# One of four layers: RWKV-7's pairs of heads in a fixed table of ticks, TensorE in program order, and the triangular inverse kept on chip

## The chip, the cores and the metric

The kernel runs on one core of one Trainium2 chip. The metric is the time of one execution in device microseconds, as the median of several executions. A profiled execution gives a trace of every instruction on the engines: TensorE (PE, with its weight loads as PEld), VectorE (DVE), ScalarE (ACT), GpSimd (POOL) and the DMA queues that SyncE (SP) feeds.

## The reference, cut to what matters

A trunk of four layers works on 512 prompt tokens and 32 sample tokens (8 sequences of 4), 544 columns in all. Its mixers are HGRN2, RWKV-7, Mamba-2 and HGRN2, and each is followed by a SwiGLU network. The change is in the second layer, RWKV-7, which has 16 heads of 64 rows:

```python
rkv = jnp.einsum('nbtd,nde->nbte', xs[:3], w_rkv)
...
def step(s, inp):
    r_t, w_t, k_t, v_t, kk_t, a_t = inp
    sa = jnp.einsum('bhvk,bhk->bhv', s, -kk_t)
    s = (s * w_t[:, :, None, :] + sa[..., None] * (kk_t * a_t)[:, :, None, :]
         + v_t[..., None] * k_t[:, :, None, :])
    return s, jnp.einsum('bhvk,bhk->bhv', s, r_t)
...
o = ((o - mean) * lax.rsqrt(var + RW_GN_EPS)).reshape(b, t, d) * lnx_w + lnx_b
bonus = jnp.sum(r * k * r_k, axis=-1, keepdims=True) * v
o = (o + bonus.reshape(b, t, d)) * gate
y = o.astype(h.dtype) @ w_out
...
x = x + out
x = x + _swiglu(_rmsnorm(x, p['norm_ffn'][i]), p['ffn_w_gate'][i], p['ffn_w_up'][i], p['ffn_w_down'][i])
```

The recurrence is computed in chunks of 64 tokens. Within a chunk the steps depend on one another through a strictly triangular 64x64 matrix for each head, and the kernel inverts one minus that matrix.

## The kernel before, in words

All activations lie with 128 of the 1024 features on partitions and tokens in columns. A product of float32 accuracy is made of three matmuls in a reduced format: a weight and an activation are each split into a high part (`whi`, `nh`) and a remainder (`wlo`, `nl`), and the products high by high, remainder by high and high by remainder are added up in PSUM. A weight tile of 128x1024 is loaded into `wraw` (three buffers), copied to `whi` by ACT (two buffers) and subtracted to `wlo` by DVE (two buffers); it then serves 24 matmuls.

The RWKV layer runs in this order. First come the projections that the keys need. Then `_rwkv_main` goes over eight objects `_Pair`: a pair is two tiles of 128 rows, hence four heads, on one half of the prompt (256 tokens, four chunks). The first four pairs are the four feature quarters of the first half, the other four those of the second half. Each pair has a `front` and a `back`:

- `front` computes `keys` for both tiles (decay scans, normalised keys, the tiles `AR` and `BKF`), the scores of keys against keys and receptances, several transposes by TensorE (`turn`), and then `inverse`. The 64x64 triangles are cut into 32x32 blocks, and these into 16x16 blocks. The 16x16 diagonal blocks go through DRAM (`nd`, then `nb`) into a layout of 64 blocks on 64 partitions, DVE solves them by 14 steps of a multiply (`pr`) and a reduction (`tb`), the result goes through DRAM again (`img`, then `TI`), and TensorE joins 16 to 32 and 32 to 64.
- `back` goes over the four chunks in a chain: products with the state carried from the chunk before, then the new state `zz` and the output `pso`. Its matmuls for output and state contract over 128 rows, in which the two kinds of rows of a head are put side by side (`SO`, `UV`, `TK`). A norm over each head (`head_norm`) and `finish` close it, tile by tile.

Beside these pairs there is work of large matmuls which does not depend on them at that time. `_rv` is the projection of receptance and value: 768 matmuls of 272 columns, needed pair by pair (line 931 of the profile). `_rwkv_end` on the first half of the prompt is the output projection and the SwiGLU network: 1776 matmuls of 256 columns (line 264), which need the first four pairs' outputs. In the text both are called products. They are emitted between the pairs in portions (`FILL`) and at a low priority, and a scheduler at build time decides by its own estimate where in each engine's queue every instruction stands. After the pairs come `_Samples` (the 32 sample tokens, with small and DVE-heavy work), the rest of the first half's products, and the tail: `_rwkv_end` on the second half with the samples, 288 columns.

Of the kernel before, what the change touches and what calls it, by code (L numbers as in the profile page):

```python
# [26 lines left out]
class Core:  # L27
# [217 lines left out]
class Part:  # L245
# [11 lines left out]
    def mm(self, w, xs):  # L257
# [19 lines left out]
    def out_proj(self, src, acts):  # L277
        for m in range(KD):
            ps = self.mm(self.k.weights(src[m], KD, P), acts)
# [16 lines left out]
    def ffn(self, layer):  # L296
# [3 lines left out]
        yield  # L300
        for g0, gn in FGRP:
            hid = []
            for m in range(g0, g0 + gn):
                ps = self.mm(k.weights(io["ffn_gate"][layer, m], KD, P), xs)
# [5 lines left out]
                yield  # L310
                ps = self.mm(k.weights(io["ffn_up"][layer, m], KD, P), xs)
                V.tensor_tensor(out=g, in0=g, in1=ps, op=ALU.mult)
                hid.append(self.halves(g, "a", m - g0))
                yield
            for m in range(KD):
                ps = self.mm(k.weights(io["ffn_down"][layer, m, :, g0:g0 + gn], gn, P), hid)
# [4 lines left out]
                yield  # L321
# [300 lines left out]
LEAD = 1  # L622
SETS = 3
FILL = (3, 2, 2, 2, 5, 3, 10, 18, 18, 18)
PRIO = 800
LOW = 4000
ENDS = 78
# [5 lines left out]
class Rwkv:  # L633
# [11 lines left out]
    def _rwkv_ffn(self, layer, rp, dp, p1, early):  # L645
        tc, nc = self.tc, self.nc
        with self.scope("rw", dict(s="01", m="2", u="e")) as pool:
# [9 lines left out]
            with tc.tile_pool(name="rw3p", bufs=1) as p3:  # L657
# [17 lines left out]
    def _rwkv_end(self, layer, part, st):  # L675
# [4 lines left out]
        yield  # L680
# [3 lines left out]
    def _rwkv_proj(self, layer, rp, p1, px, dp):  # L684
# [75 lines left out]

        z = p1.tile([P, T], F32, tag="st", name="z", bufs=3)
        G.memset(z, 0.0)
        st["img"] = []
        for j in range(8):
            t = dp.tile([8, 4, 1056], F32, name=f"img{j}")
            nc.sync.dma_start(out=t.rearrange("c b x -> (c b x)").rearrange("(p a) -> p a", p=P), in_=z[:, 0:264])
            st["img"].append(t)
# [94 lines left out]
    def _rwkv_consts(self, rp, dp):  # L862
# [7 lines left out]
        c = dict(msk=load("rmask", [P, P]), m16=load("mask16", [P, 32]), blk=load("blk", [P, P]))  # L870
# [4 lines left out]
        c["tb"] = [rp.tile([64, 16, 16], F32, name=f"tb{i}") for i in range(2)]  # L875
        for t in c["tb"]:
            nc.gpsimd.affine_select(out=t, in_=self.ones[0:64, 0:1].rearrange("p (a b) -> p a b", a=1).to_broadcast([64, 16, 16]),
                                    compare_op=ALU.is_equal, fill=0.0, base=0, pattern=[[1, 16], [-1, 16]], channel_multiplier=0)
        c["nd"] = [dp.tile([8, 4, 1056], F32, name=f"nd{i}") for i in range(3)]
        return c  # L880

    def _rwkv_main(self, layer, st, c, p2):
        carry = p2.tile([P, KD, 64], F32, name="carry")
        out = [self.xp.tile([P, T], F32, tag=f"x{m}", name="o") for m in range(KD)]
# [4 lines left out]
        proj = self._rv(st)  # L889
        end = self._rwkv_end(layer, part, st)  # L890

        def fill(gen, n):
            with self.tc.high_priority(offset=-LOW):
                for _ in range(n):
                    next(gen, None)

        for _ in range(FILL[0]):
            next(proj)
        ahead = []
        for j in range(8 + LEAD):  # L900
            if j < 8:
                ahead.append(_Pair(self, j, st, c, p2, carry))
                ahead[-1].front()
# [986 lines left out]
```

## Time and profile before

| | |
|---|---|
| Median of three executions | 3569.36 us (3558.92 to 3569.93) |
| The profiled execution | 3567.21 us, its span 3565.4 us |
| Mean granted TensorE clock, share of full speed | 0.955 |
| TensorE busy | 3357.3 us, 94% of the span |
| DVE, ACT, POOL busy | 2220.4, 1417.2 and 850.7 us |
| Pairs of the RWKV layer | 929.70 to 1413.30 us |
| Samples' chain | 1430.70 to 1527.60 us |
| Tail (second half's output projection and network) | 1593.50 to 1867.60 us |

The rows are from one profiled execution. A row with a colon between two times is a stretch of the span; the numbers behind it are its length, and for each engine busy time and (x) instructions, then the granted clock of TensorE as a share of full speed (0.5 is 1.2 GHz, 1.0 is 2.4 GHz) and the DMA's share. A row that begins with one time is an instruction or a run of alike instructions in order of time: its start, its duration, its line, what it writes and reads. Matmuls overlap, so the step from one start to the next says what one costs in a stream.

### The profile page before, as it was taken

How to read it: one execution, taken by the hardware profiler on the slowest of the kernel's cores; microseconds unless marked ns; L12 is line 12 of the kernel's file. 1: busy time of each engine (PE TensorE's matmuls, PEld its weight loads, DVE VectorE, ACT ScalarE, POOL GpSimd, SP SyncE). 2: the span in 40 equal slices, each digit the busy share in tenths (PEclk: the TensorE clock that was granted, in tenths of full speed). 3: DMA queues.
4: the chain of work that ended last, by engine and by line, in shares of the span. 5: the costliest groups of instructions: out<-in, count | busy, mean ns of one | idle time of the engine just before them, and what ended most of it. 6: DMA issues, size and time to landing. Idle time of an engine off the chain costs nothing. (4 is left out here: it accounts for less than half of the span.)

```text
span 3565.4 us, 75773 instructions
## 1 busy us (share of the span) xinstructions
PE 3357.3 (94%) x31593; PEld 3164.1 (89%) x31593; DVE 2220.4 (62%) x3714; ACT 1417.2 (40%) x2404; POOL 850.7 (24%) x930
## 2 busy tenths in 40 slices
PE   8998999999989889999998889999999999899998
PEld 7887999998877778799998778999999988799998
DVE  7787543467466665776667988763444778754345
ACT  4444422235546555245343333342223544442223
POOL 5564100022123331211003543210000466410001
PEclk9998999999968889999999989999999999899999
DMA  3222322244644323554444444332222322232223
GB/s 122 81 80 86 128 89 87 87 136 151 198 122 119 108 77 122 174 187 145 160 152 115 136 130 146 117 101 89 89 86 92 116 90 83 91 119 89 89 89 108
DMA packets 226246, 409.29 MB, mean 115 GB/s; under 512 B 66273, under 2 KB 130145, under 8 KB 225905
## 3 DMA queue, kind: packets, MB, share of 16 engines
q1 hardware_dynamic: 225904, 404.45, 35.1%
q8 instruction: 249, 4.08, 0.5%
q14 instruction: 93, 0.75, 0.1%
HBM read 357.25 MB, written 46.51 MB: 113 GB/s over the span
## 5 line engine op out<-in xcount | busy, mean ns | idle before, releaser
L62 ACT ACTIVATE whi<-wraw 128x1024 fp32r<-128x1024 f32 (+2 forms) x585 | 596.9, 1022 | 1371.3 <-issue 745.1
L64 DVE TENSOR_TENSOR wlo<-wraw,whi 128x1024 fp32r<-128x1024 f32 (+2 forms) x585 | 708.3, 1212 | 199.3 <-ACT whi L62 194.0
L93 PE MATMUL big<-nl,whi 128*128 128x256 f32 (+1 forms) x3600 | 764.5, 292 | 0.0
L93 PE MATMUL big<-nh,wlo 128*128 128x256 f32 (+1 forms) x3600 | 758.4, 291 | 2.9 <-DVE wlo L64 2.9
L93 PE MATMUL big<-nh,whi 128*128 128x256 f32 (+1 forms) x3600 | 753.7, 289 | 3.0 <-DVE raw L1482 1.8
L93 PEld LDWEIGHTS big<-nh,whi 128*128 128x128 f32 x3600 | 584.0, 190 | 11.8 <-issue 7.4
L93 PEld LDWEIGHTS big<-nl,whi 128*128 128x128 f32 x3600 | 583.4, 190 | 8.6 <-issue 7.0
L93 PEld LDWEIGHTS big<-nh,wlo 128*128 128x128 f32 x3600 | 579.7, 190 | 11.9 <-issue 6.3
L130 POOL TENSOR_TENSOR acc<-acc,sq 128x256 f32<-128x256 f32 (+1 forms) x126 | 122.0, 968 | 1663.6 <-ACT sq L129 1662.4
L212 DVE TENSOR_TENSOR fg<-fg,big 128x544 f32<-128x544 f32 x66 | 47.6, 721 | 235.4 <-PE big L93 232.9
L264 PE MATMUL psp<-nh,whi 128*128 128x256 f32 x592 | 177.0, 299 | 5.4 <-ACT whi L62 4.4
L264 PE MATMUL psp<-nh,wlo 128*128 128x256 f32 x592 | 175.9, 297 | 5.4 <-DVE wlo L64 5.2
L264 PE MATMUL psp<-nl,whi 128*128 128x256 f32 x592 | 175.3, 297 | 0.0
L208 DVE TENSOR_TENSOR fg<-big,rs 128x544 f32<-128x544 f32 x66 | 47.8, 724 | 199.4 <-PE big L93 188.7
L221 DVE TENSOR_TENSOR fd<-big,rs 128x544 f32<-128x544 f32 (+2 forms) x96 | 55.5, 580 | 176.4 <-PE big L93 159.5
L93 PE MATMUL big<-hh,wlo 128*128 128x256 f32 (+1 forms) x768 | 158.8, 288 | 0.0
L93 PE MATMUL big<-hl,whi 128*128 128x256 f32 (+1 forms) x768 | 158.1, 287 | 0.0
L93 PE MATMUL big<-hh,whi 128*128 128x256 f32 (+1 forms) x768 | 157.9, 287 | 0.0
L264 PE MATMUL psp<-x,whi 128*128 128x288 f32 x704 | 143.2, 298 | 0.0
L264 PEld LDWEIGHTS psp<-nh,whi 128*128 128x128 f32 x592 | 118.1, 199 | 11.8 <-ACT whi L62 7.0
L264 PEld LDWEIGHTS psp<-nh,wlo 128*128 128x128 f32 x592 | 118.0, 199 | 11.8 <-DVE wlo L64 7.2
L264 PEld LDWEIGHTS psp<-nl,whi 128*128 128x128 f32 x592 | 118.0, 199 | 6.2 <-issue 4.9
(620 smaller groups left out, 7390.9 us busy)
## 6 DMA issues: line engine op xcount, KB each, us to landing
wraw<-in_ffn_gate SPq DMA_DIRECT2D x110, 512.0 KB, 3.2
wraw<-in_ffn_up SPq DMA_DIRECT2D x110, 512.0 KB, 3.2
wraw<-in_ffn_down SPq DMA_DIRECT2D x80, 512.0 KB, 3.5
wraw<-in_hg_in SPq DMA_DIRECT2D x64, 512.0 KB, 3.3
wraw<-in_ffn_down SPq DMA_DIRECT2D x64, 384.0 KB, 3.1
wraw<-in_rw_in SPq DMA_DIRECT2D x40, 512.0 KB, 3.8
wraw<-in_mb_in SPq DMA_DIRECT2D x40, 512.0 KB, 3.4
wraw<-in_hg_out SPq DMA_DIRECT2D x32, 512.0 KB, 3.2
```

The source lines that it names most:

```text
L62: nc.scalar.activation(out=hi, in_=raw, func=AF.Copy)
L64: nc.vector.tensor_tensor(out=lo, in0=raw, in1=hi.bitcast(F32), op=ALU.subtract)
L93: self.nc.tensor.matmul(out=ps[0:cols, HALF[h]], lhsT=a[:, k, c0:c0 + cols], rhs=b[:, HALF[h]], start=first, stop=last)
L130: (eng or nc.gpsimd).tensor_tensor(out=acc, in0=acc, in1=sq, op=ALU.add)
L208: V.tensor_tensor(out=g, in0=pg, in1=rs, op=ALU.mult)
L212: V.tensor_tensor(out=g, in0=g, in1=pu, op=ALU.mult)
L221: V.tensor_tensor(out=d[:, c], in0=ps[:, c], in1=rs[:, c], op=ALU.mult)
L264: self.k.nc.tensor.matmul(out=ps, lhsT=a[:, i], rhs=b, start=first, stop=last)
```

## The change

Every TensorE instruction of the layer's helpers now goes through `mm`, and while `ordered` is set it is pinned in the order in which the program emits it. `_rwkv_main` emits in ten slots of 12 ticks. In slot s the `back` of pair s-2, the inverse (`inv`) of pair s-1 and the `front` of pair s each advance by one step in each tick, and behind them a tick gets its share of the products. A quantum is six matmuls. 24 quanta of the projections stand ahead of the first slot, 104 are spread over slots 0 to 5, and slots 6 to 9 get five quanta of the first half's output work in each tick. The inverse starts from the identity plus the matrix's entries inside 2x2 blocks and joins blocks of 2, 4, 8 and 16 in four rounds on chip, each of 2 times 32 matmuls of 32x32, an addition and a transpose on DVE; the two trips through DRAM and the 14 steps on 64 partitions are gone. The heads' matmuls use the 64 rows of their own head only: one K=128 product becomes two of K=64 (`SK` with `VT`, `SB` with `U`). The head norm works on both tiles at once.

```diff
+    ordered = False
+
+    def mm(self, **kw):
+
+        i = self.nc.tensor.matmul(**kw)
+        if self.ordered:
+            self.tc.keep_in_program_order(i)
...
-                self.k.nc.tensor.matmul(out=ps, lhsT=a[:, i], rhs=b, start=first, stop=last)
+                self.k.mm(out=ps, lhsT=a[:, i], rhs=b, start=first, stop=last)
+            if i % 2 and i < n - 1:
+                yield 0
...
-LEAD = 1
-SETS = 3
-FILL = (3, 2, 2, 2, 5, 3, 10, 18, 18, 18)
-PRIO = 800
 LOW = 4000
+TICKS = 12
+PROJ = (24, 6)
+PART = 5
 ENDS = 78
...
-                    for _ in range(ENDS - KD - sum(FILL[4 + LEAD:])):
-                        next(end)
-                    tail = self._rwkv_end(layer, part, st)
-                    for _ in range(KD + 2):
-                        next(tail)
-                    for _ in end:
-                        pass
-                for _ in tail:
-                    pass
+                    end.steps(ENDS - KD)
+                    tail = _Steps(self._rwkv_end(layer, part, st))
+                    tail.steps(KD + 2)
+                    end.steps(ENDS)
+                tail.steps(ENDS)
...
+        c["XI"] = [p2.tile([P, 8, 64], F32, name=f"XI{i}") for i in range(2)]
+        for t in c["XI"]:
+            self.nc.gpsimd.memset(t, 0.0)
...
-        proj = self._rv(st)
-        end = self._rwkv_end(layer, part, st)
-
-        def fill(gen, n):
-            with self.tc.high_priority(offset=-LOW):
-                for _ in range(n):
-                    next(gen, None)
-
-        for _ in range(FILL[0]):
-            next(proj)
-        ahead = []
-        for j in range(8 + LEAD):
-            if j < 8:
-                ahead.append(_Pair(self, j, st, c, p2, carry))
-                ahead[-1].front()
-            if j < 5:
-                fill(proj, FILL[1 + j])
-            if j >= LEAD:
-                ahead.pop(0).back()
-            if j >= 3 + LEAD:
-                fill(end, FILL[1 + j])
+        proj = _Steps(self._rv(st))
+        end = _Steps(self._rwkv_end(layer, part, st))
+        pairs = [_Pair(self, j, st, c, p2, carry) for j in range(8)]
+        self.ordered = True
+        proj.quanta(PROJ[0])
+        front, inv = pairs[0].front(), None
+        next(front)
+        quota = 128 - PROJ[0]
+        for s in range(10):
+            work = [g for g in (pairs[s - 2].back() if s >= 2 else None, inv, front) if g is not None]
+            front = inv = None
+            for t in range(TICKS):
+                for g in work:
+                    next(g, None)
+                if t == 7 and s < 7:
+                    front = pairs[s + 1].front()
+                    next(front)
+                n = s * TICKS + t
+                if s < PROJ[1]:
+                    proj.quanta(quota * (n + 1) // (PROJ[1] * TICKS) - quota * n // (PROJ[1] * TICKS))
+                else:
+                    end.quanta(PART)
+            for g in work:
+                for _ in g:
+                    pass
+            if s < PROJ[1] <= s + 1:
+                proj.quanta(128)
+            if s < 8:
+                inv = pairs[s].inv()
+                next(inv)
+        self.ordered = False
...
+                        if k in (1, 3, 5):
+                            yield 0
                     t = self.tmps("sq", 3)[:, 0:RV]
                     nc.scalar.copy(out=t, in_=ps)
                     nc.sync.dma_start(out=st[name][m][:, cols], in_=t)
-                yield
+                    yield 1
...
+            ps = [psb("s", [P, 4, 2, 64]) for _ in range(2)]
+            for a in (1, 0):
+                for q, e in each:
+                    mm(out=flat(ps[a][rows[e], q]), lhsT=BK[rows[e], q, a], rhs=flat(AR[rows[e], q]), start=True, stop=True)
+            SW = [til(f"SW{a}", [P, 4, 64]) for a in range(2)]
+            for a in (1, 0):
+                V.tensor_tensor(out=SW[a], in0=ps[a][:, :, 0], in1=mask(0), op=ALU.mult)
+            for a, t in ((1, self.SK), (0, self.SB)):
+                V.tensor_tensor(out=t[:, i], in0=ps[a][:, :, 1], in1=mask(64), op=ALU.mult)
...
-        for b in range(4):
-            nc.sync.dma_start(out=rowsof(nd, b), in_=NNf[quarter[b]])
-        nb = til("nb", [nb_, 16, 16], 2)
-        nc.sync.dma_start(out=nb, in_=blocks(nd))
-        tb = c["tb"][self.j % 2]
-        V.tensor_copy(out=tb[:, 1, 0:1], in_=nb[:, 0:1, 1])
-        for t in range(2, 16):
-            pr = til("pr", [nb_, 15, 15], 2)
-            V.tensor_tensor(out=pr[:, 0:t, 0:t], in0=nb[:, 0:t, t].rearrange("p (o j) -> p o j", o=1).to_broadcast([nb_, t, t]),
-                            in1=tb[:, 0:t, 0:t].rearrange("p j s -> p s j"), op=ALU.mult)
-            V.tensor_reduce(out=tb[:, t, 0:t], in_=pr[:, 0:t, 0:t], axis=mybir.AxisListType.X, op=ALU.add)
-        nc.sync.dma_start(out=blocks(img), in_=tb)
-        TI = til("TI", [P, n2, 32], 2)
-        for b in range(4):
-            nc.sync.dma_start(out=TI[quarter[b]], in_=rowsof(img, b))
...
+        M = til("ML", [P, 4, n2, 32])
+        X, TI = til("X", [P, n2, 32], 2), til("TI", [P, n2, 32], 2)
+        G.tensor_tensor(out=X, in0=flat(self.NN), in1=c["lmask"][:, 1:2].to_broadcast([P, n2, 32]), op=ALU.mult)
+        G.tensor_tensor(out=X, in0=X, in1=c["lmask"][:, 0:1].to_broadcast([P, n2, 32]), op=ALU.add)
+        G.tensor_tensor(out=M, in0=flat(self.NN).rearrange("p (o c) t -> p o c t", o=1).to_broadcast([P, 4, n2, 32]),
+                        in1=c["lmask"][:, 2:6].rearrange("p l (o t) -> p l o t", o=1).to_broadcast([P, 4, n2, 32]), op=ALU.mult)
+        V.transpose(out=lines(TI), in_=lines(X))
...
-        Y = til("Y", [P, n2, 32], 2)
-        ACT.copy(out=Y, in_=quads(M, TI, own))
-        V.tensor_tensor(out=X, in0=X, in1=quads(Y, X, own), op=ALU.add)
-        T32 = TI
-        V.transpose(out=T32.rearrange("p c t -> p (c t)"), in_=X.rearrange("p c t -> p (c t)"))
+        for l in range(4):
+            Y = til("Y", [P, n2, 32], 2)
+            ACT.copy(out=Y, in_=quads(M[:, l], TI, own))
+            yield
+            V.tensor_tensor(out=X, in0=X, in1=quads(Y, X, own), op=ALU.add)
+            V.transpose(out=lines(TI), in_=lines(X))
+            if l < 3:
+                yield
...
+            for i in range(2):
+                for x, a, first in ((VT, 1, True), (U, 0, False)):
+                    for e in range(2):
+                        mm(out=pp[rows[e], i], lhsT=TK[rows[e], i, q, a], rhs=x[rows[e], i, q], start=first, stop=not first)
...
+                terms = [(VT[:, i, q], self.SK[:, i, q]), (U[:, i, q], self.SB[:, i, q])]
                 if z is not None:
...
-                for i, e in both:
-                    PE.matmul(out=pp[rows[e], i], lhsT=TK[e][:, i, q], rhs=UV[e][:, i, q], start=True, stop=True)
...
-                        PE.matmul(out=po[rows[e], i, q], lhsT=UV[e][:, i, q], rhs=SO[e][:, i, q], start=True, stop=z is None)
```

On TensorE, this is a place in the fourth of the pair slots after the change (`L75` is the helper `mm`; `psp` takes a product, `zz,XA` is the chain of `back`, `TI,ML` a round of the inverse, `bn,blk` the bonus sum of `front`):

```order
L75 MATMUL psp<-nh_9646,wlo 128x272
L75 MATMUL psp<-nl_9647,whi 128x272
L75 MATMUL psc<-zz,XA 64x64 x4
L75 MATMUL psm<-TI,ML 32x32 x32
L75 MATMUL pss<-bn,blk 128x256
L75 MATMUL psp<-nh_9648,whi 128x272
L75 MATMUL psp<-nh_9648,wlo 128x272
L75 MATMUL psp<-nl_9649,whi 128x272
```

The same kinds of work in the kernel before, where a pair's chain and another pair's inverse meet (`L1183`, `L1188`, `L1196` and `L1199` are the chain, `L1141` the inverse, `L1057` scores, `L264` a product):

```order
L1183 MATMUL psc<-zz,XA 64x64 x4
L1141 MATMUL psm<-TI,NN 32x32 x3
L952 MATMUL pss<-bn,blk 128x256
L1141 MATMUL psm<-TI,NN 32x32 x22
L1196 MATMUL pso<-SO_12939,UV_12943 64x64
L1141 MATMUL psm<-TI,NN 32x32 x4
L1188 MATMUL psc<-UV_12943,TK_12941 64x64
L1188 MATMUL psc<-UV_12944,TK_12942 64x64
```

A stage of the inverse that was cut up by the chain's matmuls stands in one piece after the change, behind the chain's step and ahead of the tick's products, and nothing can pass a matmul whose input is late.

On DVE, this is the start of one pair's 14 steps in the kernel before (`pr` and `tb`), with other pairs' work between:

```order
L1120 COPY tb_10730<-nb 64x1
L1014 SCALAR_TENSOR_TENSOR kn<-lk,rvec,rk 128x256
L1123 TENSOR_TENSOR pr<-nb,tb_10730 64x2x2
L1125 TENSOR_REDUCE tb_10730<-pr 64x2
L1123 TENSOR_TENSOR pr<-nb,tb_10730 64x3x3
L1125 TENSOR_REDUCE tb_10730<-pr 64x3
L1123 TENSOR_TENSOR pr<-nb,tb_10730 64x4x4
L968 TENSOR_TENSOR fd<-fd,fs 128x256
```

After the change, at the place where the projections turn from the first 272 columns to the next (`nl` is the remainder of a new input, `X` and `TI` are the inverse, `zz` the chain, `wlo` a weight's remainder):

```order
L1217 TENSOR_TENSOR zz<-zd,psc 128x128
L1054 SCALAR_TENSOR_TENSOR bn<-lr,rvec,la 128x256
L69 TENSOR_TENSOR nl_9649<-sq,nh_9648 128x272
L1157 TENSOR_TENSOR X<-X,psm 128x256
L69 TENSOR_TENSOR nl_9651<-sq,nh_9650 128x272
L1158 STREAM_TRANSPOSE TI<-X 128x256
```

The short steps are replaced by one addition and one transpose for each round; at the turn of the projections the sixteen remainders stand among the steps of the inverse and the chain.

## Rows read from the trace of the kernel before

**Rows 1.** Four stretches: the pairs, the last pair's finish, the samples, the remaining products.

```profile
929.70:1413.30 483.60, 433.95 (x5534) 372.12 (x5535) 301.10 (x749) 268.83 (x559) 138.33 (x243) 0.82 0.42 120
1413.30:1430.70 17.40, 13.20 (x97) 11.68 (x96) 9.22 (x18) 10.02 (x14) 6.57 (x8) 1.00 0.41 130
1430.70:1527.60 96.90, 90.18 (x814) 73.26 (x815) 76.04 (x115) 31.14 (x45) 31.37 (x37) 0.95 0.56 180
1527.60:1593.50 65.90, 62.95 (x508) 61.78 (x507) 45.22 (x72) 29.05 (x42) 2.61 (x7) 0.97 0.55 187
```

**Rows 2.** The pairs' stretch from 991.60, cut where the granted clock changes.

```profile
991.60:1104.30 112.70, 100.86 (x1327) 83.36 (x1326) 67.12 (x185) 56.94 (x135) 26.26 (x53) 0.62 0.40 107
1104.30:1189.60 85.30, 76.46 (x1046) 64.19 (x1044) 59.14 (x148) 54.73 (x115) 32.71 (x52) 0.98 0.44 125
1189.60:1346.60 157.00, 136.94 (x1896) 114.33 (x1895) 97.33 (x270) 85.59 (x182) 55.51 (x89) 0.75 0.33 89
1346.60:1413.30 66.70, 63.87 (x796) 58.92 (x796) 40.43 (x75) 39.08 (x62) 8.51 (x12) 1.00 0.38 123
```

**Rows 3.** Two of these stretches, TensorE's instructions of line 931 (projections) alone.

```profile
991.60:1104.30 112.70, 32.05 (x129) 25.40 (x129) 0.62 0.40 107
1104.30:1189.60 85.30, 36.46 (x228) 30.90 (x228) 0.98 0.44 125
```

**Rows 4.** TensorE in order of time, clock full, small work and then products.

```profile
1348.51 0.75 PE L1141 MATMUL psm<-TI,NN 32*32 32x32 f32 x64
1349.19 0.70 PE L952 MATMUL psu<-o,blk 128*128 128x256 f32 x2
1349.54 0.47 PE L264 MATMUL psp<-nh,whi 128*128 128x256 f32 x1
1349.85 0.28 PE L264 MATMUL psp<-nh,wlo 128*128 128x256 f32 x1
1349.96 0.28 PE L264 MATMUL psp<-nl,whi 128*128 128x256 f32 x1
1350.08 0.28 PE L264 MATMUL psp<-nh,whi 128*128 128x256 f32 x1
```

**Rows 5.** The same products just before, at half clock.

```profile
1344.88 0.41 PE L264 MATMUL psp<-nh,whi 128*128 128x256 f32 x1
1345.10 0.41 PE L264 MATMUL psp<-nh,wlo 128*128 128x256 f32 x1
```

**Rows 6.** TensorE in order of time, clock full, three runs of 64x64 matmuls.

```profile
1253.47 0.68 PE L947 MATMUL pss<-ident,lv 64*64 64x64 f32 x16
1254.08 0.38 PE L264 MATMUL psp<-nh,whi 128*128 128x256 f32 x1
...
1367.08 1.15 PE L1095 MATMUL psm<-XI,AT 64*64 64x64 f32 x32
1368.16 0.48 PE L952 MATMUL psu<-fs,blk 128*128 128x256 f32 x1
...
1248.06 0.33 PE L1199 MATMUL pso<-R,zz 64*64 64x64 f32 x4
1248.32 0.34 PE L1196 MATMUL pso<-SO,UV 128*64 128x64 f32 x4
```

**Rows 7.** Groups of DVE instructions in the pairs' stretch: busy, mean, idle before.

```profile
L64 DVE TENSOR_TENSOR wlo<-wraw,whi 128x1024 fp32r<-128x1024 f32 x53 | 65.9, 1243 | 32.9 <-ACT whi L62 31.7 <-PE pss L1071 1.2
L1123 DVE TENSOR_TENSOR pr<-nb,tb 64x4 f32<-64x4 f32 (+6 forms) x112 | 41.7, 372 | 2.2
L1125 DVE TENSOR_REDUCE tb<-pr 64x2 f32<-64x4 f32 (+6 forms) x112 | 26.1, 233 | 2.0
```

**Rows 8.** Groups of ACT instructions in the pairs' stretch.

```profile
L68 ACT ACTIVATE nh<-sq 128x272 fp32r<-128x272 f32 (+1 forms) x23 | 9.4, 420 | 9.5 <-DMA sq<-dxr 5.9 <-DMA sq<-dxv 3.6
```

**Rows 9.** Groups of DVE and TensorE instructions in the samples' stretch.

```profile
L64 DVE TENSOR_TENSOR wlo<-wraw,whi 128x1024 fp32r<-128x1024 f32 x20 | 27.4, 1369 | 3.7 <-ACT whi L62 3.6
L264 PE MATMUL psp<-nh,whi 128*128 128x256 f32 x152 | 45.3, 298 | 2.7 <-ACT whi L62 1.7 <-DVE sq L312 1.0
```

More of the change, by code (lines that the diff above doesn't have):

```diff
@@ L930, in _rv @@
                         for a, b, first, last in ((w[0], xh, k == 0, False), (w[1], xh, False, False), (w[0], xl, False, k == KD - 1)):
-                            nc.tensor.matmul(out=ps, lhsT=a[:, k], rhs=b, start=first, stop=last)
+                            self.mm(out=ps, lhsT=a[:, k], rhs=b, start=first, stop=last)
+                        if k in (1, 3, 5):
+                            yield 0
                     t = self.tmps("sq", 3)[:, 0:RV]
@@ L934, in _rv, with __init__, quanta, steps @@
                     nc.sync.dma_start(out=st[name][m][:, cols], in_=t)
-                yield
+                    yield 1
+class _Steps:
+    def __init__(self, gen):
+        self.gen, self.done = gen, 0
+    def quanta(self, n):
+        for _ in range(n):
+            self.done += next(self.gen, 0)
+    def steps(self, upto):
+        while self.done < upto:
+            try:
+                self.done += next(self.gen)
+            except StopIteration:
+                break
 class _Work:
@@ L1038, in front @@
[L1038 to L1039 removed]
+        nc, c, til, psb, mm = self.k.nc, self.c, self.til, self.psb, self.k.mm
+        V, ACT, G = nc.vector, nc.scalar, nc.gpsimd
+        rows = ROWS
         four = lambda tag, bufs: til(tag, [P, 2, 4, 64], bufs)
[L1041 to L1043 removed]
@@ new lines, in front @@
+        keys = self.keys(0)
+        yield
+        self.NN, self.N12 = (til(n, [P, 2, 4, 32], 2) for n in ("NN", "N12"))
+        self.W, self.AT = four("W", 2), four("AT", 2)
+        self.SB, self.SK, self.VT, self.R = (four(n, 3) for n in ("SB", "SK", "VT", "R"))
+        self.TK = til("TK", [P, 2, 4, 2, 64], 3)
+        each = [(q, e) for q in range(4) for e in range(2)]
+        flat = lambda t: t.rearrange("p a t -> p (a t)")
+        mask = lambda a: c["msk"][:, a:a + 64].rearrange("p (o t) -> p o t", o=1).to_broadcast([P, 4, 64])
@@ new lines, in front @@
+        for i in range(2):
+            AR, BK, v, bn = keys
+            ps = psb("s", [P, 4, 64])
+            for q, e in each:
+                self.turn(ps[rows[e], q], v[rows[e], 64 * q:64 * q + 64], e)
+            ACT.copy(out=self.VT[:, i], in_=ps)
+            yield
+            ps = [psb("s", [P, 4, 2, 64]) for _ in range(2)]
+            for a in (1, 0):
+                for q, e in each:
+                    mm(out=flat(ps[a][rows[e], q]), lhsT=BK[rows[e], q, a], rhs=flat(AR[rows[e], q]), start=True, stop=True)
[4 more added lines that the diff above has]
+                V.tensor_tensor(out=t[:, i], in0=ps[a][:, :, 1], in1=mask(64), op=ALU.mult)
@@ L1085, in front @@
                 self.turn(ps[rows[e], q], AR[rows[e], q, 0], e)
-            ACT.copy(out=AT[:, i], in_=ps)
-            G.tensor_tensor(out=self.R[:, i], in0=AR[:, :, 1], in1=dec[:, 0:4].rearrange("p (c o) -> p c o", o=1).to_broadcast([P, 4, 64]), op=ALU.mult)
-        self.inverse(NN, N12)
-        XI = self.XI
-        each = [(i, q, e) for i in range(2) for q in range(4) for e in range(2)]
-        ps = psb("m", [P, 2, 4, 64])
-        for i, q, e in each:
-            PE.matmul(out=ps[rows[e], i, q], lhsT=AT[rows[e], i, q], rhs=XI[rows[e], 4 * i + q], start=True, stop=True)
@@ L1200, in back @@
-                z = new
-        for i in range(2):
-            ACT.copy(out=oo[i], in_=po[:, i].rearrange("p c t -> p (c t)"))
-        last = self.til("zd", [P, 2, 64], 2) if h else self.carry[:, 2 * self.p:2 * self.p + 2]
+                        mm(out=po[rows[e], i, q], lhsT=a[rows[e]], rhs=b[rows[e]], start=a is terms[0][0], stop=a is terms[-1][0])
+            z = new
+            if q < 3:
+                yield
+        O = til("O", [P, 512])
+        ACT.copy(out=O, in_=po.rearrange("p i c t -> p (i c t)"))
```

248 lines of the change are left out of this document (115 added, 133 removed).

## Prediction

> **What bounds the kernel now.** I first read the whole span: TensorE is busy for 94% of it, so what counts is how many matmuls there are, at what clock, and with what gaps. The change touches one layer, so next I cut that layer into stages by the table of stretches [rows 1]. The reader is to see that these four stages run end to end from 929.70 to 1593.50 us, 663.8 us in all, and that only the first runs at a granted clock of 0.82; the three behind it are at 0.95 to 1.00. What stands ahead of 929.70 and the tail behind 1593.50 hold the same matmuls before and after, so I make the sum on these 663.8 us alone.
>
> In the first stage TensorE is idle for 483.6 - 433.95 = 49.7 us, a tenth. The clock costs more. It has two levels, 1.2 and 2.4 GHz, and a stretch with a mean of 0.82 has spent a share 2 x (1 - 0.82) = 0.36 of its time on the lower one, 174 us; the same cycles at full clock take half of that, so about 87 us are lost. The same stage cut finer [rows 2] shows where: 0.62 for 112.7 us and 0.75 for 157 us, against 0.98 and 1.00 in the two others. TensorE's busy share is no guide to it: it is 89% and 87% where the clock is low, 90% and 96% where it is high. What differs is the number of large products. In the stretch at 0.62 there are 129 projections in 112.7 us, 1.1 per us, and in the stretch at 0.98 there are 228 in 85.3 us, 2.7 per us [rows 3]. Where the heads' small matmuls stand alone, the clock falls.
>
> So two stages matter: the pairs, bounded by TensorE at a reduced clock, and the samples, where DVE is busy for 76.0 of 96.9 us [rows 1], 27.4 us of that with the weight splits of products that run beside it [rows 9].
>
> **The change part by part.** First the unit prices at full clock.
> - A product of 256 columns: 1349.85 to 1350.08 is 0.23 us for two [rows 4], so 0.118 with the rounding of the rows; of 272 columns, by columns, 0.126. At half clock it is 0.22 [rows 5].
> - 32 matmuls of 32x32 leave 64 records, and 1348.51 to 1349.19 is 0.68 us [rows 4].
> - A run of eight 64x64 matmuls (16 records) takes 0.61, one of 32 records 1.08 to the next start [rows 6], so 0.034 a record in a run.
> - Where the shape of the tile changes, time is lost: four records at 0.034 should take 0.14 and take 0.26 [rows 6], 0.12 more; and the first product behind small work takes 0.31 instead of 0.12 [rows 4], 0.19 more. The mean is 0.15.
>
> *TensorE's work from 929.70 on, after.* All 768 projections: 768 x 0.126 = 97 us. Of the first half's 1776 products, 1398 now stand in the slots (by the order of the changed program): 1398 x 0.118 = 165 us. A tile's front has three runs of eight 64x64 (0.61 each), one of 16 (1.08), the scores on their own rows (32 records of 128 columns, twice the 64-column price, 2.1) and the bonus (0.35 [rows 4]), together 5.4, and a pair has two: 10.8. The inverse has 8 stages of 0.68, two of 0.61 and two of 1.08: 8.8. The back has 32 records in a chunk of the first half and 48 in one of the second, at 0.034, with two changes of shape, so 1.35 and 1.9, for four chunks 6.5 on the mean, and 1.4 for the norm's two sums of 512 columns, each twice the 0.35 that one of 256 takes [rows 4]: 7.9. That is 27.5 a pair, 220 us for eight. These prices hold some 30 changes of shape a pair; the order after shows 408 in the slots, 168 more, at 0.15: 25 us. Sum: 97 + 165 + 220 + 25 = 507 us.
>
> *The on-chip inverse.* The 224 short DVE steps, 41.7 + 26.1 = 67.8 us of DVE time [rows 7], go; 24 additions and 32 transposes come, each like one that the stage has (about 0.43 us), 24 us. TensorE had waited little for that chain, since others' work stood behind it. So I cost it at nothing on the path; what it frees is room on DVE for the splits and additions of 1398 - 581 products that move into this stage.
>
> *The samples' stretch.* Before, 456 products ran in it and 508 behind it [rows 1, 9]; after, 138 stand ahead of it or at its start and 96 inside, and the last 144 stand behind the tail's norm, where before 136 stood. So 222 products fewer run in the stretch: 222 x 0.118 = 26 us of TensorE, which was busy for 90 of the 97 us, and half of the splits' 27.4 us on DVE with about as much again in the additions behind the products. I take 97 - 26 = 70, and 6 for the finish ahead of it and the hand-over: 76 us. Bounds: 50 + 6 (DVE's own work alone, 76 less those 28, rounded up) and 97 + 6 (the length is the chain's own, and nothing is gained).
>
> *Gain before stalls:* 663.8 - 507 - 76 = 81 us.
>
> *Clock.* Slots 0 to 5 hold 104 quanta of six in some 6 x 40 us, 2.6 products per us, as in the stretch at 0.98 [rows 3]; slots 6 to 9 hold 350 products each. So I expect a nearly full clock and take 12 us of loss, for the first slot and the turn of the projections. Bounds: 0 and 0.18 x 507 = 91 us.
>
> *Program order.* This is the cost. Each of the 120 ticks holds a chain's step, a stage of the inverse, a step of a front, then products, and none can pass another. Behind a late matmul stand the tick's products, and behind these all that DVE and ACT would get next. The wait to reckon with is DVE's queue: a stage of the inverse needs an addition and a transpose (0.86 us), and if a weight's split (1.24 us [rows 7]) has just begun, that comes first. A tick lasts about 4 us with 1 to 4 us of products as cover. Three terms:
> - the turn of the projections: 16 inputs are loaded, rounded on ACT and subtracted on DVE, about 0.45 us each, and ACT already idles for 9.5 us there for DMA [rows 8]; TensorE now cannot go on to a pair: 10 us;
> - slot 6, where the first half's output work begins with its inputs' split and, behind the output projection, a norm: 10 us;
> - the remaining ticks, 0.2 us each: 22 us.
> Together 42 us; bounds 25 (a tenth idle, as now [rows 1], on the 245 us of small work) and 100 (rival 1).
>
> *Sum.* -81 + 12 + 42 = -27 us. Against the profiled execution's own 3567.2 (span 3565.4, so 1.8 us lie around it) that is 3540. The median of the runs shown is 2.2 us above that execution, and two of the three lie within 3 us of it; I leave it at 3540.
>
> **A rule against the change.** The row says 0.12 to 0.19 us for a change of shape [rows 4, 6]. The Trainium skill, TensorEngine Tiling (Array Packing), Key Properties, says that changing the tiling mode drains TensorE. If a drain were a whole product's recorded 0.28 us for each of the 408 changes rather than 0.15, the sum would be 53 us worse. The rows include whatever drain there is, so I stay with them.
>
> **The rivals.**
> 1. *Stalls of program order eat the gain (slower).* Place: the slots' ticks, where TensorE waits for DVE. After the clock's 12 us, 69 us are left, so it decides at 69 / 120 = 0.58 us per tick. If in two of three ticks TensorE stands behind a weight split of 1.25 us, that is 100 us: 3567 - 69 + 100 = 3598. For it: DVE is busy for 62% of the stage now and stays near that, and its queue is in order. Against it: products cover most of a tick in slots 6 to 9. Chance 0.17.
> 2. *The stalls are covered.* With 15 us in all and a full clock: 3567 - 81 + 15 = 3501. For it: the steps of a tick belong to different pairs, so each has a whole tick for its answer. Chance 0.20.
> 3. *The samples' stretch stays.* If its length is the chain's latency and not DVE's load, it stays near 97 and the sum is 27 us worse: 3567, no change that can be told. For it: DVE there idles for 21 us. Chance 0.12.
> 4. *The clock does not come back.* If it stays at 0.82, 91 us are lost instead of 12: 3619. For it: short gaps in every tick. The Trainium skill, TensorE: Matmul & The Clock Gate, in A second HAM failure mode, tells of a kernel whose clock swung because TensorE idled briefly and often; no run here shows that yet, and in the stretch at 0.98 TensorE idles for as large a share as in the one at 0.62 [rows 2]. Chance 0.06.
> My forecast, a gain of about 27 us, has 0.45.
>
> **How the numbers follow.** The range has to take in rival 2's 3501, with a few us for a samples' stretch nearer its lower bound, and on the other side part of rival 1: with stalls of 87 us instead of 100 it is 3585. I take 3495 to 3585, which leaves out rival 4 and the upper half of rival 1. A difference of 0.3% (10.7 us) is about what a measurement can tell from no change. Faster: 0.43 of the forecast's 0.45, 0.20 of rival 2 and 0.05 of rival 3 (a stretch a little shorter than 97): 0.68. Same: 0.02 of the forecast, 0.07 of rival 3 and 0.05 of rival 1, 0.14. Slower: 0.12 of rival 1 and 0.06 of rival 4, 0.18.
>
> **What would show it.** Right: the stage of the pairs lasts 540 to 580 us from 929.70 and holds nearly all products, its granted clock is above 0.95, the samples follow in about 75 us and the tail starts near 1567 instead of 1593.50. Waits of TensorE for DVE's `X`, `TI` or `wlo` sum to some 40 us, the largest single ones at the turn of the projections. Wrong: a clock below 0.9 in slots 0 to 5 (rival 4), TensorE idle for over a fifth of them (rival 1), or a samples' stretch above 90 us (rival 3).

## The result, and the profile after

The changed kernel is slower: 3620.49 us (3613.39 to 3629.83, four executions) against 3569.64 us, a ratio of 1.0145 with a 95% interval of 1.0107 to 1.0182. The prediction had 3540 and a gain.

The table of stretches of the changed kernel, with the columns of [rows 1]: the whole of pairs, samples and what lies between, then its two parts, then the tail. The samples' chain begins at 1542.50, when the last pair's output is written, and the tail's first product starts at 1634.80.

```profile
929.70:1634.80 705.10, 600.18 (x11163) 530.47 (x11161) 398.66 (x706) 303.90 (x575) 183.92 (x250) 0.92 0.40 124
929.70:1542.50 612.80, 540.02 (x10617) 488.56 (x10616) 348.12 (x622) 284.40 (x545) 157.86 (x212) 0.94 0.39 122
1542.50:1634.80 92.30, 60.17 (x548) 41.91 (x546) 50.54 (x85) 19.49 (x31) 26.06 (x38) 0.79 0.46 138
1634.80:1909.50 274.70, 264.35 (x1944) 260.56 (x1944) 182.98 (x278) 125.26 (x189) 21.31 (x25) 0.98 0.47 153
```

The same stretch was 663.8 us before, and the four rows of [rows 1] add up to 600.28 us of TensorE. After, TensorE is busy for 600.18 us, the same. So in the balance of this one trace the 41.3 us that this part got longer are idle time: 63.5 us before, 104.9 after. Behind that equality two changes cancel. The clock came back in part, from a loss of some 94 us (the shares below 1.00 of [rows 1] times their lengths) to 0.08 x 705.1 = 56 us. But the matmuls themselves grew by about as much: by this estimate 600 - 94 = 506 us at full clock before, 600 - 56 = 544 after. (Idle time loses nothing to a low clock. With the shares times the busy time of each stretch the losses are 84 and 45 us, and the work is 516 and 555: the growth, 38 or 39 us, is the same.) The tail has its old length. From the tail's start to the end of the span it is 3620.5 - 1634.8 = 1985.7 us, before 3565.4 - 1593.5 = 1971.9: 13.8 us more lie behind the layer.

Who waited for whom in the changed kernel, TensorE, from 900 to 1640 us (total, times, longest; the ten largest):

```profile
PE psp L75 <- DVE wlo L64: 14.4, 9, 3.1
PE psp L75 <- ACT a L68: 11.0, 1, 11.0
PE psm L75 <- DVE XA L1188: 8.7, 2, 4.4
PE psp L75 <- ACT nh L68: 8.6, 6, 3.0
PE psm L75 <- ACT U L1183: 8.4, 4, 3.1
PE psu L75 <- ACT fs L984: 6.8, 2, 4.6
PE pss L1382 <- DVE s L1383: 6.3, 3, 2.5
PE psm L75 <- ACT Y L1155: 5.3, 4, 3.0
PE psc L75 <- DVE zz L1217: 5.2, 2, 3.5
PE psu L1361 <- DVE WO L1355: 4.7, 1, 4.7
```

But for one, no single wait is longer than 4.7 us; there are many kinds. The exception is the second row, the end of the samples' chain: TensorE stood 11 us until the tail's inputs came. `XA` and `U` (17 us) are waits by a matmul that needs neither value: it writes the inverse's one PSUM bank (`psm`), and DVE or ACT has yet to read that bank out. TensorE in order of time behind one of them, and then in the samples' chain:

```profile
1026.92 1.08 PE L75 MATMUL psm<-TI,ML 32*32 32x32 f32 x64 [4.40 <-DVE XA L1188]
1027.93 1.12 PE L75 MATMUL pss<-ident,lv 64*64 64x64 f32 x16
1028.98 0.59 PE L75 MATMUL psp<-nh,whi 128*128 128x272 f32 x1
...
1592.12 1.91 PE L1361 MATMUL psu<-WO,SS 32*32 32x64 f32 x32 [4.69 <-DVE WO L1355]
1595.61 1.92 PE L1361 MATMUL psu<-X,SS 32*32 32x64 f32 x32 [1.57 <-DVE X L1364]
1599.08 1.92 PE L1361 MATMUL psu<-X,SS 32*32 32x64 f32 x32 [1.56 <-DVE X L1364]
```

Behind the wait of 4.40 us the 64 records take 1.01 us to the next start, not the 0.68 of [rows 4]. The granted clock ahead of the wait and behind it:

```profile
1015.00:1022.50 7.50, 5.36 (x84) 4.76 (x84) 1.65 (x4) 3.28 (x7) 2.44 (x4) 1.00 0.28 94
1026.90:1031.50 4.60, 4.58 (x91) 4.42 (x92) 0.00 (x0) 0.74 (x2) 0.00 (x0) 0.50 0.36 118
```

So this wait is paid twice, once as idle time and once at the lower clock. And between 1592 and 1602 TensorE and DVE hand the samples' chain to each other with no product between.

Why `XA` came so late, DVE shows in the first three rows; the last four are ACT ahead of a `U` for which TensorE waited 3.1 us until 1135.29:

```profile
1024.56 0.48 DVE L1054 SCALAR_TENSOR_TENSOR bn<-lr,rvec,la 128x256 f32<-128x256 f32 x1 [5.49 <-DMA db<-bn]
1024.96 1.22 DVE L64 TENSOR_TENSOR wlo<-wraw,whi 128x1024 fp32r<-128x1024 f32 x1
1026.09 0.68 DVE L1188 TENSOR_TENSOR XA<-psm,dec 128x512 f32<-128x512 f32 x1
...
1130.33 1.28 ACT L987 ACT_TABLE_LOAD   x1 [0.92 <-DVE fv L986]
1132.54 1.28 ACT L988 ACT_TABLE_LOAD   x1
1133.83 0.63 ACT L988 ACTIVATE fs<-fs 128x512 f32<-128x512 f32 x1
1134.67 0.57 ACT L1183 COPY U<-psm 128x512 f32<-128x512 f32 x1
```

DVE had stood for 5.49 us until a DMA had read an earlier `bn`, whose buffer the next one takes, and then a weight's split came first. ACT had two table loads of 1.28 us for another pair's head norm in its queue. The bank is where TensorE stops; what makes the answer late lies in the queues of DVE and ACT. No run took the DMA of `bn` or the table loads away, so what they cost in time is not shown.

### The profile page after: what moved, and what is told of

It is laid out like the page before. It is cut to its first block, busy times and chain, and to the rows that moved or that the text cites. A ratio compares the mean times of both kernels' runs of the same rounds, so it can differ in the third digit from the quotient of the medians.

```text
span 3620.5 us, 83616 instructions
## 1 busy us (share of the span) xinstructions
PE 3365.0 (93%) x35785; PEld 3182.9 (88%) x35785; DVE 2187.0 (60%) x3470; ACT 1384.6 (38%) x2326; POOL 849.8 (23%) x897
## 4 chain that ended last, share of the span: by engine, by line
PE 48%; DVE 8%; DMA 3%; issue 2%; ACT 2%; POOL 1%; SPq 0%; POOLq 0%; DVEq 0%; ACTq 0%
PE big L101 27%; PE psp L75 11%; PE big L91 5%; DVE wlo L64 2%; DMA E<-cumd 1%; DVE E L1585 1%; DVE sq L1529 1%; PE psm L75 1%; ACT whi L62 1%; PE pss L75 1%; DVE sq L1531 0%; DMA out_wkv_s<-s 0%; PE psc L75 0%; DVE ql L502 0%; PE pso L75 0%
## 5 line engine op out<-in xcount | busy, mean ns | idle before, releaser
L75 PE MATMUL psp<-nh,whi 128*128 128x256 f32 (+1 forms) x848 | 265.0, 312 | 10.3 <-ACT nh L68 8.6
L75 PE MATMUL psp<-nh,wlo 128*128 128x256 f32 (+1 forms) x848 | 249.8, 295 | 14.4 <-DVE wlo L64 14.4
L75 PE MATMUL psp<-nl,whi 128*128 128x256 f32 (+1 forms) x848 | 249.5, 294 | 0.7 <-DVE nl L69 0.7
L75 PEld LDWEIGHTS psp<-nh,whi 128*128 128x128 f32 x848 | 168.0, 198 | 24.4 <-ACT nh L68 10.1
L75 PEld LDWEIGHTS psp<-nh,wlo 128*128 128x128 f32 x848 | 168.7, 199 | 18.2 <-DVE wlo L64 16.3
L75 PEld LDWEIGHTS psp<-nl,whi 128*128 128x128 f32 x848 | 168.2, 198 | 2.3 <-DVE nl L69 1.2
L75 PE MATMUL psp<-x,whi 128*128 128x288 f32 x704 | 141.0, 295 | 0.0
```

The lines of the kernel that those rows point to most:

```text
L75: i = self.nc.tensor.matmul(**kw)
```

## The experiments

Two theories stood at first. A: the samples' chain has a length of its own, and the change took the products from beside it. B: the loss is the waits of the pinned program order. C, the rival to A, is the prediction's own reason: the products' DVE work sets the samples' length. D and E came with e5: the inverse on chip costs by its matmuls (D), or it pays by what it frees on DVE (E). Ratios are to the kernel before on the same chip, with 95% intervals.

**Products per tick (e1, e2, e3).** One number moves products between the late slots and the samples.

```diff
-PART = 5
+PART = 4      (e1; 3 in e2, 7 in e3)
```

> The changed kernel, with four quanta a tick in place of five in the last four slots, so that 48 quanta (288 products) stand beside and behind the samples instead of ahead of them. Theory A (the samples' chain has a length of its own, some 92 us, and TensorE has too little to do beside it: in the changed kernel it is busy for 60 of 92.3 us at a clock of 0.79): 288 x 0.118 = 34 us leave the slots and come back as next to nothing, so the time falls from 3620 to about 3590. Theory B (waits of program order are the whole loss): only the slots' waits for weight splits change, within 10 us of 3620. Theory C (the products' DVE work sets the samples' length): 12 more weights with their splits and additions lengthen the stretch by about 25 us, so about 3611.

> Three quanta a tick, as near as the table comes to the split of the kernel before: 576 products (68 us at full clock) leave the slots. Theory A: the samples' stretch has room for some 32 us of idle time and 19 us that the low clock takes, about 51 us in all; what does not fit runs behind it. Time about 3570, and no better with still fewer in the slots. Theory B: within 10 us of 3620. Theory C: about 3600.

> Seven quanta a tick: all 1776 products of the first half stand in the slots, none beside the samples. It measures the samples' chain alone. Theory A: the chain still takes 85 to 92 us, the slots grow by 348 x 0.118 = 41 us, less the products gone from behind: time about 3640 to 3660. Theory C (forecast's reason): the chain falls to 70 us or less, and the time stays within 10 us of 3620.

Measured: e1 1.0087 (1.0060 to 1.0114), e2 1.0077 (1.0059 to 1.0095), e3 1.0231 (1.0205 to 1.0257); with the change's 1.0145 that is 3650, 3620, 3598 and 3594 us for seven, five, four and three. The stretch from the last pair's output to the tail's start in e1, e2 and e3, from the tables of stretches:

```profile
1518.20:1618.10 99.90, 87.45 (x814) 69.71 (x813) 76.66 (x118) 31.95 (x45) 31.27 (x38) 0.96 0.60 184
```
```profile
1479.70:1608.40 128.70, 120.11 (x1076) 103.25 (x1075) 96.96 (x155) 48.02 (x71) 31.40 (x42) 0.96 0.62 190
```
```profile
1601.20:1676.60 75.40, 38.37 (x358) 19.96 (x358) 32.40 (x56) 7.11 (x13) 25.64 (x38) 0.66 0.38 99
```

With seven (the last row) there is no product in it: 358 records are the samples' own. So the chain alone takes 75.4 us; with 548 - 358 = 190 products beside it 92.3, with 456 99.9, and with 718 128.7. From none to 190 products it grows by 17 us, a part of what C says; from 190 to 456 by 8, while 266 products are 31 us of TensorE; from there on every product is paid in full (262 more, 29 us). A is right about the time: between 21 and 27 us of the 51 are the split, by the ratios and medians of e1 and e2. Its guess that the chain alone is 85 us or more was wrong.

**Order not pinned (e4).**

```diff
-        self.ordered = True
+        self.ordered = False
```

> The changed kernel with TensorE's program order not pinned (the flag stays off); the emission order is the same and the scheduler places by its own estimate. Theory B (the stalls of program order, 71 us idle in the slots against 50 before, and the clock that falls in them, are what is lost): TensorE's idle time in the pairs falls to 50 us or less and the time to 3580 or less. Theory A: the stretch beside the samples is untouched, and the time changes by less than 20 us, either way; the clock may fall again where small matmuls gather, as before.

Measured: 1.0096 (1.0067 to 1.0124), 3601.5 us, 19 us better than the change. The pairs and the samples:

```profile
929.70:1527.20 597.50, 547.61 (x10604) 491.22 (x10603) 349.52 (x621) 283.99 (x547) 160.87 (x222) 0.94 0.40 125
1527.20:1617.70 90.50, 61.38 (x548) 41.19 (x546) 49.54 (x85) 19.29 (x31) 26.20 (x38) 0.78 0.47 141
```

Idle time in the pairs is 49.9 us instead of 72.8, at the same clock and with 8 us more of busy time, and the samples' stretch stays as it was. B is right that the pin adds idle time (23 us) and wrong that it is the whole loss: it expected 3580 or less. So A and B each hold a part, in different stretches. By itself this difference, 1.0096 against 1.0145, is at the edge of what the intervals can tell; with three quanta (e2 against e10) it is larger and clear.

**The inverse alone, in the kernel before (e5).** Four rounds of joined blocks in place of DRAM and the 14 DVE steps, nothing else changed.

```diff
-        for b in range(4):
-            nc.sync.dma_start(out=rowsof(nd, b), in_=NNf[quarter[b]])
...
-        ACT.copy(out=Y, in_=quads(M, TI, own))
-        V.tensor_tensor(out=X, in0=X, in1=quads(Y, X, own), op=ALU.add)
+        for l in range(4):
+            Y = til("Y", [P, n2, 32], 2)
+            ACT.copy(out=Y, in_=quads(M[:, l], TI, own))
+            V.tensor_tensor(out=X, in0=X, in1=quads(Y, X, own), op=ALU.add)
+            V.transpose(out=lines(TI), in_=lines(X))
```

> The kernel before with one part of the change alone: the inverse by four rounds of joined blocks on chip, in place of the trips through DRAM and the 14 DVE steps; pairs, order and heads as before. Theory D (the change adds TensorE work: in the traces a pair's own matmuls cost 196 / 8 = 24.5 us at full clock before and 243 / 8 = 30.3 after, and six more stages of 0.68 us each are 4.1 of that): 8 x 4.1 = 33 us more of small matmuls, partly at half clock, so 20 to 45 us slower than before, 3590 to 3615. Theory E (DVE's 44 us less and the missing waits for DRAM outweigh it, since the scheduler fills gaps): within 10 us of before, or faster. My forecast costed this part at nothing on the path beyond its matmuls.

Measured: 1.0086 (1.0060 to 1.0112), 3599.9 us: 30 us slower, as D has it. The row of its whole stretch, to the tail's start, and the same row of the kernel before:

```profile
929.70:1623.30 693.60, 616.08 (x10020) 534.88 (x10021) 406.98 (x769) 347.42 (x682) 193.25 (x309) 0.90 0.42 125
929.70:1593.50 663.80, 600.27 (x6948) 518.84 (x6949) 431.58 (x953) 339.05 (x658) 178.88 (x293) 0.86 0.45 135
```

At full clock that is 616 - 0.10 x 694 = 547 us of matmuls, 41 more than before. The inverse alone would account for the 38 us by which TensorE's work grew in the change. With it the granted clock is higher, too, 0.90 against 0.86, so a part of the clock that came back came with these small matmuls.

**A second bank for the inverse (e6, e7).** On top of three quanta a tick, the inverse's tile takes the head norm's bank in turn with its own; e7 also lifts the pin.

```diff
-        with self.scope("rw", dict(s="01", m="2", u="e")) as pool:
+        with self.scope("rw", dict(s="01", m="2e", u="e")) as pool:
```

> Three quanta a tick, and the inverse's PSUM tile takes two banks in turn (its own and the one that the head norm's sums use) instead of one. In the trace of the changed kernel TensorE waits 8.4 us for U and 8.7 us for XA in places where the waiting matmul needs neither, only their bank. Theory B' (program order turns the one bank into stalls, and each long stall is followed by a stretch at half clock): these 17 us go, and of the 41 us that the clock costs in the slots some 10 more, so about 25 us better than 3594: 3569. Rival: the waits move to the shared bank (DVE's and ACT's reading of the norm's sums) or to the next input that is late: within 8 us of 3594.

> The one before, with the program order not pinned. If the pinned order costs what idle time it adds (23 us of idle time less and 9 us more of matmul time in the run without it), about 14 us better than the pinned one of this pair. If the two banks have already taken the long waits away, no difference beyond 5 us.

Measured: e6 1.0131 (1.0099 to 1.0162), 20 us slower than e2; e7 1.0041 (1.0023 to 1.0058). In e6 the waits for TensorE over the pairs are led by these:

```profile
PE psm L75 <- DVE fv L986: 17.7, 7, 4.5
PE psu L75 <- ACT fs L984: 8.6, 5, 3.4
```

The rival is right on the place: the waits moved to the shared bank, seven of them for the norm's `fv`. It had the time within 8 us of e2; the loss of 20 us is more than either theory allowed. Lifting the pin is worth 29 us here, twice what was expected, and about the same 0.9% as without the second bank (e2 against e10, below).

**The kernel before once more (e8).**

> The kernel before once more, for a second trace. Of the changed kernel's 55 us, 13 stand behind this layer, where both programs hold the same work (1695 us from the tail's end to the last instruction before, 1708 after, and 1703 to 1709 in the four kernels tried so far). If this is the spread of executions, the second trace shows 1700 or more; if it belongs to the change, about 1695 again.

Measured: one execution, 3565.2 us. Its stretch from 929.7 to the tail ends at 1585.0 in a span of 3563.5, so 1978.5 us lie behind, between the 1971.9 and the 1985.7. So two executions of the same kernel differ here by 6.6 us. In the runs with the change's slots it is 3598.3 - 1617.7 = 1980.6 us in e4, also 1980.6 in e10, 1985.9 in e12 and 1990.0 in e9, and in e5, which has the order of before, 1973.6. So a part of the 13.8 us is spread, and a part of some us seems to come with the slots; its cause stays open.

**The old inverse in the slots (e9, e11, e12).** DRAM, DVE steps and one round of joining are put back as steps of the same slots: with the change as it is, with three quanta, and with three quanta and no pin.

```diff
-        G.tensor_tensor(out=X, in0=flat(self.NN), in1=c["lmask"][:, 1:2].to_broadcast([P, n2, 32]), op=ALU.mult)
+        for b in range(4):
+            nc.sync.dma_start(out=rowsof(nd, b), in_=NNf[quarter[b]])
...
+            if t in (7, 11, 14):
+                yield
+        nc.sync.dma_start(out=blocks(img), in_=tb)
```

> The changed kernel with the inverse of before put back (two trips through DRAM, 14 steps on DVE, one round of joining 16 to 32) as steps of the same slots; five quanta a tick, program order pinned. Theory D (the joined blocks add some 41 us of small matmuls, which the run with that part alone showed as 30 us): about 30 us better than 3620, 3590. Rival (in pinned order the trips through DRAM and 8.5 us of short DVE steps a pair come late, and all behind them waits): 3620 or slower.

> Old inverse and three quanta a tick, program order pinned. If inverse and quanta add up (30 and 27 us): 3563, level with before. If the old inverse makes the pinned order wait: 3580 or slower.

> Old inverse, three quanta a tick, program order not pinned: what is left of the change is the slots as an emission order, heads on their own rows and the norm of 512 columns. If all three effects add up (30, 27 and 19 us): 3545, faster than before by some 0.7%. If the clock falls back to what before shows (85 us lost in the pairs) once the small matmuls of the joined blocks are gone: 3570 or slower.

Measured: e9 1.0139 (1.0114 to 1.0164), no different from the change; e11 1.0057 (1.0031 to 1.0083); e12 0.9970 (0.9950 to 0.9990). The whole stretch of e9 and the waits that lead in its pairs:

```profile
929.70:1631.90 702.20, 577.15 (x8106) 509.72 (x8105) 429.02 (x891) 296.90 (x552) 165.03 (x242) 0.89 0.44 130
```
```profile
PE pss L75 <- ACT VT L1091: 16.3, 5, 6.8
PE psm L75 <- DMA TI<-img: 13.8, 4, 11.3
PE psm L75 <- ACT U L1211: 12.4, 3, 6.7
```

At full clock TensorE's work is 577 - 0.11 x 702 = 500 us, 44 less than in the change. Of that about 21 us come back through the clock (0.89 against 0.92) and 20 as idle time, so the length stays within 3 us. In pinned order the matmuls that the inverse no longer needs turn into waits, for the trip through DRAM (`img`, 13.8 us) and for answers of ACT (16.3 and 12.4 us); that the chain of answers then sets the length is my reading, not shown apart. Without the pin e12 lies 0.2% under e10, below, which the intervals do not tell apart.

**Three quanta and no pin (e10).** The two edits of e2 and e4 together.

> The changed kernel with three quanta a tick and program order not pinned, one PSUM bank for the inverse as in the change. If the two effects measured apart add up (27 us for the quanta, 19 for the order): about 3575. If the second bank did the work in the run that had all three (3585): 3594 or slower.

Measured: 0.9991 (0.9974 to 1.0008), as fast as before. The whole stretch of e10, and of e12:

```profile
929.70:1589.40 659.70, 593.69 (x11142) 524.34 (x11141) 400.51 (x709) 303.42 (x579) 194.56 (x263) 0.95 0.43 132
```
```profile
929.70:1571.10 641.40, 566.80 (x8045) 498.83 (x8044) 425.01 (x892) 293.86 (x551) 169.41 (x247) 0.93 0.48 139
```

The two effects add up, and to a little more: 1.0145 falls to 0.9991, by 0.0154, where 27 and 19 us of 3570 make 0.0129. Undoing the split of the products and the pin together takes the whole loss away, with the inverse on chip, the heads on their own rows and the joint norm still in e10. Against e7 (1.0041) it also shows that the second bank cost time with the order free, too. e12, and e15 below, beat both kernels, by 0.3% against before. The heads on their own rows and the joint norm are in every version with the slots, and no run takes them apart, so their share is not known.

**In which slots the pin costs (e13, e14), and fewer products yet (e15).** The pin held in slots 0 to 5 only, or in 6 to 9 only, with three quanta; and e12 with two.

```diff
+            self.ordered = s < PROJ[1]       (e13; s >= PROJ[1] in e14)
...
-PART = 3
+PART = 2                                 (e15)
```

> The changed kernel with three quanta a tick; program order pinned in slots 0 to 5 only, free in slots 6 to 9. In the trace of the changed kernel most of the waits over half a microsecond that the pinned order leaves, and nearly all of the clock's loss, lie in slots 0 to 5, where a tick has one or two quanta as cover. If these slots hold the cost, this kernel stays within 6 us of the one pinned throughout (1.0077 of before). If the late slots hold it, it comes near 0.9991.

> The counterpart: free in slots 0 to 5, pinned in slots 6 to 9. If the early slots hold the cost of the pinned order, this kernel comes near the free one (0.9991 to 1.002 of before). If the late slots hold it, near 1.0077.

> The fastest version so far (old inverse, program order free, 0.997 of before) with two quanta a tick. Its samples' stretch is already filled (TensorE idle for 8 of 125 us), so the 288 products more that leave the slots run behind the samples at full price, while the slots keep fewer products beside the heads' small matmuls: equal or up to 15 us slower, 0.997 to 1.001. If the late slots were still crowded, it would be faster, 0.994 or less.

Measured: e13 1.0060 (1.0041 to 1.0080), e14 1.0040 (1.0023 to 1.0056), between the 1.0077 of the full pin and the 0.9991 of none. Each half costs something and their intervals overlap, so in which slots the pin costs more stays open. e15 is 0.9975 (0.9957 to 0.9994), as e12: from three quanta to two nothing is gained or lost.

## Why the prediction was wrong, point by point

The prediction's sum for 929.7 to the tail's start was 507 of matmuls, 12 of clock, 42 of program order and 76 for the samples, 637 us. Measured, by the rows above: 540.0 - 37 = 503 of matmuls in the pairs' stretch, 0.06 x 612.8 = 37 of clock, 612.8 - 540.0 = 73 idle, and 92 for the samples, 705. The difference of 68 us and the 13.8 behind the layer make the 81 us between 3540 and 3621. The step that failed is the size of the stalls: clock and program order stood at 12 and 42 us and came to 37 and 73, 56 us of the 68. The samples' stretch adds 16, and the work takes 4 away.

Where the clock's loss lies, two rows show: the instructions that write `psp`, nearly all of them products, to 1260 us and behind it.

```profile
929.70:1260.00 330.30, 126.23 (x730) 0.91 0.39 121
1260.00:1542.50 282.50, 189.13 (x1439) 0.98 0.38 124
```

- **TensorE's work** was right: 507 against 503. The prices of the runs of small matmuls, with 0.15 us for a change of shape, hold as a sum; no run tests one of them alone. The inverse's matmuls stood in this sum, so they are not the error. What I did not do is the same sum for before: 506 us with the samples, against 544 after. It shows that the gain rested on the clock: of some 82 us that the clock was to give back, from 94 to 12, the added work took 38 from the start (the inverse alone 41, e5). With 38 us of clock regained instead of 82, nothing was left for the stalls. One count on DVE was off without effect: 24 transposes come with the inverse, not 32.
- **The samples' stretch** failed: 76 expected, 92.3 measured. I subtracted the missing products in proportion. The chain alone takes 75 us (e3), and with 190 products it is already at 92, so taking 266 products away from the 456 of before shortened the stretch by 5 us (96.9 to 92.3), where I had counted 26, and TensorE idled. The rival that named this ("its length is the chain's latency") had 0.12, and its sign, a stretch above 90 us, came. By the medians, moving 288 products back (e1) gave 23 us, 576 (e2) 27.
- **Program order** failed in size: 42 expected, 73 measured, inside the bounds of 25 to 100 and above the 69 at which rival 1 decides. So rival 1 came, in the place that it named, but not by the wait that it named: the weight split stands with 14.4 us, and most of the rest are other late answers and the inverse's one PSUM bank. The 42 was also less than the 49.7 us that stood idle in the pairs before, where nothing was pinned, and I gave no reason why a pinned order should leave less. The same emission without the pin leaves 49.9 (e4); the pin adds 23. With three quanta, lifting it takes the time from 1.0077 to 0.9991 (e2, e10).
- **The clock** failed in size: 12 expected, 37 measured. The direction was right (0.82 became 0.94). The reason that I gave counted on 2.6 products per us in slots 0 to 5, at 40 us a slot. The 104 quanta of these slots ran from 946 to 1254 us, 51 us a slot. With those ahead of the first slot that is 2.2 products per us to 1260 us, at a clock of 0.91, and then 5.1 at 0.98, by the two rows above; so the loss lies where the slots took longer than I had them. I had also not joined the clock to the stalls, though it fell behind the wait at 1022 us. That the two are one thing is not shown: in e4 the idle time fell by 23 us and the clock of the pairs stayed at 0.94. How much of the 25 us that I had too little each of them makes stays open. The 87 us that the prediction has as lost in the pairs before count idle time, too; over busy time, 0.18 x 434, they are 78. Rival 4, a clock that stays at 0.82, did not come.
- **Behind the layer** 13.8 us came, of which a second trace of before shows 6.6 (e8). I had taken this part as fixed.
- **The dearer change of shape**, 0.28 us instead of 0.15 and 53 us in all, was rightly set aside: the work came out 4 us below the sum.

## What to carry to other kernels

Sum the busy time at full clock for before as well as for after: a better clock that comes with more small matmuls can leave busy time exactly where it was. Independent work is worth most beside a serial chain that has nothing else to cover it; measure how long such a stage is without its cover (e3) before taking the cover away. A pinned order needs every answer in time; try the same emission order without the pin first, here worth 0.5 to 0.9% in four pairs of kernels. Where a matmul waits for a bank, look at what the engine that empties the bank was itself waiting for, before giving it a second one.

## What the runs showed of the hardware

A wait of 4.4 us in front of small matmuls was followed by a stretch at a granted clock of 0.50, after 1.00 ahead of it, in which 64 records of 32x32 took 1.01 us instead of 0.68. With the samples' chain alone and TensorE busy for 38 of 75 us the granted clock was 0.66, and with 456 products beside it 0.96. In this program a PSUM bank counts as a dependency of its own: with one bank for all steps of the inverse, 17 us of TensorE's waits stood in front of it, and taking the norm's bank in turn with it made the kernel 0.5% slower, pinned (e6 against e2) and free (e7 against e10). The head norm's two table loads on ACT took 1.28 us each.
